# First expert in 64 slots with unsplit products and its rows in two halves, alone, then three split blocks to two of pairs

## The chip, the cores and the metric

The kernel runs on one core of a Trainium2 chip. The metric is the device time of one execution in microseconds (us). Before the change the median of three runs is 1375.55 us (1373.21 to 1376.93). TensorE is called PE here, VectorE DVE, ScalarE ACT, GpSimd POOL, and SP is the engine whose queue issues nearly all loads.

## What is computed

Two decoder layers over 256 positions of width 1024 in float32. The even layer is two kinds of attention and a dense SwiGLU. The odd layer is a mixture of dilated attentions and then a mixture of experts, which is where the change lies:

```python
def expert_block(args):
    xb, e = args
    return (jax.nn.silu(xb @ w1[e]) * (xb @ w3[e])) @ w2[e]
```

A router takes for each of the 256 positions the two experts of eight with the highest logits; each expert is a SwiGLU of inner width 3584 over the positions that chose it, and the two results are summed with the softmax of the two logits. Every expert's w1 and w3 are 1024x3584 and w2 is 3584x1024, so all eight hold 352 MB, and each word is needed once. With the reference's own inputs the router sends 63, 71, 67, 71, 63, 63, 60 and 54 rows to experts 0 to 7 (worked out by running the reference).

## The kernel before

**Places and slots.** After the router the experts are sorted by their row counts, the largest first, but expert 0 is always put at place 0, because its weights can then be loaded before the router has answered (`picked(0)` names `W[n][0]`; for other places SP reads the expert's number into a register). `CAP` gives the slots of each place: 128 for places 0 to 3, 64 for places 4 to 7. An expert with more rows than slots is finished by `overflow`, a loop under an If that is not entered with these counts.

**Blocks.** An expert's work is cut into seven blocks of 512 inner columns. A block needs six weight tiles of 1 MB: two of w1, two of w3 (each 4 x 128 rows by 512 columns), two of w2 (2 x 128 rows by 1024). `load` takes the next of twelve slots in a fixed round (six of the `raw` pool, then buffers that the attention has left, listed in `late`) and issues the DMA on SP; the DMA waits until that slot's last reader is done.

**Two kinds of blocks.** A *split* block (places 0 to 3, 128 slots) writes each weight as hi + lo: ACT rounds a row of 1024 to `hi` (line 222), DVE takes the rest to `lo` (line 223), and PE makes three matmuls of it (`mm3`, lines 232 to 234). Only five pairs of hi and lo exist (`WB=5`). A *pair* block takes two experts of 64 slots at once (`up2`, line 285; `down`, line 651): unsplit float32 matmuls straight from the raw tiles, one expert on columns 0 to 63 of the array and one on columns 64 to 127, side by side. Each such matmul stands twice in a trace.

**Order.** `swiglu` walks the list `items`. For each item it makes x.w1, takes silu on ACT (line 700), finishes the item before (transposes in `gate_T`, then w2 in `down`), makes x.w3 and multiplies on DVE (line 713). The list is split, split, pair, fourteen times; the last pair block is cut into two of 256 columns. Before an expert's first block `begin` gathers its rows with one-hot matrices (lines 973 and 979), after its last `combine` scatters them back. `overflow` stands in item 26.

**Ahead.** Expert 0's first two w1 tiles are loaded and split during the attention of the odd layer by `ahead`, with POOL doing the subtraction.

Of the kernel before, what the change touches and what calls it, by code (L numbers as in the profile page):

```python
# [7 lines left out]
F32 = mybir.dt.float32  # L8
# [30 lines left out]

CAP = (128, 128, 128, 128, 64, 64, 64, 64)  # L40
FIRST = 1 << 20
# [111 lines left out]
def trunk(ctx: ExitStack, tc: tile.TileContext, a, out, R=6, WB=5, NF=16):  # L153
# [462 lines left out]
    def swiglu(items, ws, between=None, behind=None, next_ws=None, tail=None, rare=None):  # L616
# [22 lines left out]
        def down(it, gs, fill=iter(())):  # L639
            w1, w3, w2, c0, n, sta, accs, first, last, pre, post = it  # L640
            nr = n // P
            accs = accs()
            if isinstance(w1, tuple):
# [14 lines left out]
                return  # L658
            for r in range(0, nr, 2) if not last else [0]:
                ws = []  # L660
                m = 1 if tail and it is items[-1] else 2
                for q in range(r, nr if last else r + 2, m):
                    v = load(w2, c0 // P + q, m, 0, D)
                    ws += [split(v[:, j:j + 1, :]) for j in range(m)]
# [13 lines left out]
        for it in items:  # L678
# [13 lines left out]
            two = isinstance(w1, tuple)  # L692
            u = up2(p1[0], w1, c0, n, sta[0]) if two else up(p1, w1, c0, n, sta, ws, between)
            step(u, 2)
            if prev:
# [3 lines left out]
            for q, p in zip(s, p1):  # L699
                A.activation(q[:, :n], p[:, :n], AF.Silu)  # L700
            held = tail and it is items[-1]
            if prev and not held:
                down(prev[0], gs)
            if rare and it is items[26]:
                rare()
            p3 = [wk() for _ in sta]
            with tc.issue_after(behind) if ws else nullcontext():
                end(up2(p3[0], w3, c0, n, sta[0]) if two else up(p3, w3, c0, n, sta))
            ws = None
            if held:  # L710
                down(prev[0], gs)
            for q, p in zip(s, p3):
                V.tensor_mul(q[:, :n], q[:, :n], p[:, :n])  # L713
            prev = (it, s)
# [97 lines left out]
    for i, m in enumerate(mms):  # L812
        TE.matmul(pc[:, :8], lhsT=upb[:, P:], rhs=m, start=i == 0, stop=i == len(mms) - 1)
    over, place = [cp.tile([P, 8], F32, name=q) for q in ("over", "place")]
    tmp = fa("tmp")
# [14 lines left out]
    with tc.issue_after(behind):  # L830
# [6 lines left out]
        V.tensor_copy(number, place[0:1, :])  # L837
        V.tensor_tensor(over, m8, cst[:, C_LIM:C_LIM + 8], op=ALU.is_gt)
        V.tensor_reduce(mx, over[0:1, :], axis=AX, op=ALU.max)
        V.tensor_copy(most, mx)  # L840
# [40 lines left out]
    state = {}  # L881

    new_y = lambda: xp.tile([P, 2, D], F32R, tag="x", name=nm("y"), bufs=2)

    def overflow():

        ws = [raw() for _ in range(2)]
        fs = [fa("more") for _ in range(4)] + [fb("more") for _ in range(2)]
        ys, m = new_y(), fs[3]
        with tc.If(nc.values_load(most, min_val=0, max_val=1) > 0):  # L890

            nth, n = [m[:, 8 * i:8 * i + 8] for i in range(2)]
            V.tensor_copy(n[:, 0:1], over[:, 0:1])
            for i in range(1, N_EXP):
                V.tensor_add(n[:, i:i + 1], n[:, i - 1:i], over[:, i:i + 1])
# [5 lines left out]
    def more(nth, m, wa, xg, wd0, wd1, g, _, fo, fg, ys):  # L901
# [3 lines left out]
        one, t, col, t2 = [m[:, 8 * i:8 * i + 8] for i in range(4)]  # L905
        V.tensor_scalar(one, nth, 1.0, None, op0=ALU.is_equal)

# [13 lines left out]
        pick(col[:, 5:6], t2)  # L921
        for h in range(2):
            pick(col[:, h:h + 1], slots[h])
# [41 lines left out]

    def gather(qs):

        n = len(qs) * P
        oneh = fb("oneh")[:, :2 * n].rearrange("p (h j s) -> p h j s", h=2, s=P)
        for h in range(2):  # L970
            for j, q in enumerate(qs):
                s = slot0[h][:, 0:1] if q == 0 else slots[h][:, q:q + 1]
                V.tensor_scalar(oneh[:, h, j, :], iota, s, None, op0=ALU.is_equal)
        xg = []
        for k in range(KT):
            ps = wk()
            for i, xs in enumerate((xh, xl)):
                for h in range(2):
                    TE.matmul(ps[:, i * n:(i + 1) * n], lhsT=xs[h][:, k * P:(k + 1) * P],
                              rhs=oneh[:, h].rearrange("p j s -> p (j s)"), start=h == 0, stop=h == 1)  # L980
            yield
            if k * n % T == 0:
                t = fb("xg")
            v = t[:, k * n % T * 2:][:, :2 * n]
            (A.copy if k % 2 else V.tensor_copy)(v, ps[:, :2 * n])
            xg.append(v.rearrange("p (a s) -> p a s", a=2))
        for j, q in enumerate(qs):
            ssl = slice(j * P, (j + 1) * P)
            state["sta", q] = [lambda k, ssl=ssl: (xg[k][:, 0, ssl], xg[k][:, 1, ssl])]
            state["oneh", q] = oneh[:, :, j, :]  # L990

# [20 lines left out]

    def begin(qs):

        if CAP[qs[0]] == 64:
            yield from gather2(qs[0])
        elif ("sta", qs[0]) not in state:
            yield from gather(qs)
        q = qs[0]
        n = P // CAP[q]  # L1020
        state["ot", q] = by_slot(state["oneh", q], [g[:, q:q + n, :].rearrange("p a b -> p (a b)") for g in gg], n,
# [40 lines left out]
    def picked(q):  # L1062
# [11 lines left out]
        return [Picked(n, a[n], ROWS[n], at) for n in ("odd_w1", "odd_w3", "odd_w2")]  # L1074


    def expert(q):
        end_ = q == 6
        ch = [(c, 512) for c in range(0, D_FFE, 512)]
        if end_:  # L1080
            ch[-1:] = [(D_FFE - 512, 256), (D_FFE - 256, 256)]
        ws3 = list(zip(picked(q), picked(q + 1))) if CAP[q] == 64 else picked(q)
        for i, (c, n) in enumerate(ch):
            first, last = i == 0, i == len(ch) - 1
            pre = None
            if first:
                pre = lambda: begin([q])
            elif (q, i) == (0, 1):
                pre = residual
            yield (*ws3, c, n, lambda: state["sta", q], lambda: e_acc(q), first, last, pre,  # L1090
                   (lambda: combine(q, end_)) if last else None)
# [62 lines left out]
```

## Time and profile before

| what | value |
|---|---|
| median of the runs | 1375.55 us |
| the profiled execution's own time | 1373.32 us |
| its span (first to last instruction) | 1371.6 us |
| busy: PE, DVE, ACT | 1300.7, 784.7, 614.1 us |
| mean HBM traffic over the span | 310 GB/s |
| first matmul of the experts | at 470.12 us |
| last weight tile landed | by 1350 us (2 GB/s from there to 1357.5 us) |

Times inside a trace are us from the span's start. A span is read with care: PE counts as busy while matmuls overlap, so a PE at 95% is not a PE at its peak. The experts take from 470 us to the end, and the DMA engines move all their weights in that time, so both have to be read by stretches.

### The profile page before, as it was taken

To read this page: it belongs to the slowest core of one execution; us is meant where nothing else is said; L and a number is where in the kernel's file an instruction comes from. 1 tells how busy PE (TensorE), PEld (TensorE's weight loads), DVE (VectorE), ACT (ScalarE), POOL (GpSimd) and SP (SyncE) were. 2 spreads that over 40 slices of the span, in tenths; PEclk is the share of its full clock that TensorE was granted. 3 is DMA by queue.
4 is the path that set the end of the run, shared out by engine and by line. 5 is a ranking of instruction groups with operands and counts; after the bars stand their busy time and mean duration, and the time that the engine had idled before them with its cause. 6 is when DMAs were issued, how large, how long until landed. Compare 5 with 4: busy or idle time off the path is not lost. (4 is left out here: it accounts for less than half of the span.)

```text
span 1371.6 us, 16690 instructions
## 1 busy us (share of the span) xinstructions
PE 1300.7 (95%) x6130; PEld 886.3 (65%) x6130; DVE 784.7 (57%) x1201; ACT 614.1 (45%) x859; POOL 53.7 (4%) x40
## 2 busy tenths in 40 slices
PE   9998999999999899999999999999979999999996
PEld 7776888887777775564746556466646475646562
DVE  6988445547777574453645455464625474644463
ACT  5564434443555364453444445254525353544441
POOL 0012000101022100000000000000000000000001
PEclk9999999999999699999999999999999999999998
DMA  9532456654445489999999999997999998999964
GB/s 371 193 110 98 161 184 222 224 194 158 154 148 184 168 308 399 422 419 422 408 376 422 419 421 404 384 359 288 423 366 384 416 412 346 420 420 421 401 230 168
DMA packets 69191, 426.23 MB, mean 311 GB/s; under 512 B 7920, under 2 KB 16368, under 8 KB 19824
## 3 DMA queue, kind: packets, MB, share of 16 engines
q1 hardware_dynamic: 68096, 421.70, 78.0%
q0 software_dynamic: 864, 3.15, 0.7%
q8 instruction: 50, 0.82, 0.2%
q14 instruction: 37, 0.30, 0.1%
q10 hardware_dynamic: 144, 0.26, 0.1%
HBM read 424.03 MB, written 1.05 MB: 310 GB/s over the span
## 5 line engine op out<-in xcount | busy, mean ns | idle before, releaser
L223 DVE TENSOR_TENSOR lo<-raw,hi 128x1024 fp32r<-128x1024 f32 (+1 forms) x454 | 535.0, 1219 | 236.6 <-ACT hi L222 235.7
L222 ACT ACTIVATE hi<-raw 128x1024 fp32r<-128x1024 f32 (+2 forms) x472 | 467.1, 1034 | 230.6 <-PE wk L234 124.1
L285 PE MATMUL wk<-raw,xg 128*64 128x512 f32 (+1 forms) x960 | 213.1, 575 | 5.5 <-PEq L890 5.3
L233 PE MATMUL wk<-lo,xg 128*128 128x512 f32 x448 | 177.8, 397 | 5.3 <-DVE lo L223 5.2
L232 PE MATMUL wk<-hi,xg 128*128 128x512 f32 x448 | 178.3, 398 | 0.5 <-DVE x L1057 0.5
L234 PE MATMUL wk<-hi,xg 128*128 128x512 f32 x448 | 175.2, 391 | 0.0
L713 DVE TENSOR_TENSOR sl<-sl,wk 128x512 f32<-128x512 f32 (+1 forms) x55 | 36.3, 666 | 227.3 <-PE wk L285 139.3
L285 PEld LDWEIGHTS wk<-raw,xg 128*64 128x64 f32 x960 | 69.2, 138 | 128.1 <-issue 121.6
L232 PE MATMUL acc<-hi,gh 128*128 128x512 f32 x312 | 118.5, 400 | 15.1 <-ACT hi L222 14.5
L233 PE MATMUL acc<-lo,gh 128*128 128x512 f32 x312 | 122.7, 395 | 4.7 <-DVE lo L223 4.7
L234 PE MATMUL acc<-hi,gl 128*128 128x512 f32 x312 | 121.6, 392 | 1.4 <-DVE gl L635 1.2
L232 PEld LDWEIGHTS wk<-hi,xg 128*128 128x128 f32 x448 | 84.4, 188 | 37.2 <-issue 19.5
L233 PEld LDWEIGHTS wk<-lo,xg 128*128 128x128 f32 x448 | 84.4, 188 | 26.3 <-DVE lo L223 8.9
L651 PE MATMUL acc<-raw,gt 128*64 128x512 f32 x448 | 100.9, 598 | 0.3 <-ACT gt L626 0.3
L234 PEld LDWEIGHTS wk<-hi,xg 128*128 128x128 f32 x448 | 84.4, 188 | 16.9
L700 ACT ACTIVATE sl<-wk 128x512 f32<-128x512 f32 (+1 forms) x55 | 32.0, 582 | 138.4 <-PE wk L285 74.3
L232 PEld LDWEIGHTS acc<-hi,gh 128*128 128x128 f32 x312 | 58.0, 188 | 36.5 <-ACT hi L222 22.0
L232 PE MATMUL wk<-hi,xT 128*128 128x512 f32 (+1 forms) x192 | 72.4, 377 | 0.3 <-ACT xT L315 0.3
L233 PEld LDWEIGHTS acc<-lo,gh 128*128 128x128 f32 x312 | 58.6, 188 | 21.7 <-DVE lo L223 9.4
L233 PE MATMUL wk<-lo,xT 128*128 128x512 f32 (+1 forms) x192 | 71.7, 373 | 0.0
L234 PE MATMUL wk<-hi,xT 128*128 128x512 f32 (+1 forms) x192 | 71.5, 373 | 0.0
L651 PEld LDWEIGHTS acc<-raw,gt 128*64 128x64 f32 x448 | 35.2, 137 | 54.7 <-issue 54.0
(208 smaller groups left out, 1359.3 us busy)
## 6 DMA issues: line engine op xcount, KB each, us to landing
raw<-in_odd_w SPq DMA_DIRECT2D x326, 1024.0 KB, 9.6
raw<-in_even_w SPq DMA_DIRECT2D x31, 1024.0 KB, 4.9
raw<-in_odd_w_in SPq DMA_DIRECT2D x12, 1024.0 KB, 4.8
raw<-in_odd_w SPq DMA_DIRECT2D x20, 512.0 KB, 5.4
raw<-in_even_w_in SPq DMA_DIRECT2D x8, 1024.0 KB, 11.7
raw<-in_even_w_out SPq DMA_DIRECT2D x4, 1024.0 KB, 5.4
raw<-in_odd_w_out SPq DMA_DIRECT2D x4, 1024.0 KB, 5.2
raw<-in_even_w SPq DMA_DIRECT2D x4, 512.0 KB, 3.6
```

The source lines that it names most:

```text
L222: A.activation(hi, v, AF.Copy)
L223: by.tensor_sub(lo, v, hi.bitcast(F32))
L232: TE.matmul(o, lhsT=sh, rhs=wh, start=first, stop=False)
L233: TE.matmul(o, lhsT=sh, rhs=wl, start=False, stop=False)
L234: TE.matmul(o, lhsT=sl, rhs=wh, start=False, stop=last)
L285: TE.matmul(o[i * 64:(i + 1) * 64, :ncol], lhsT=sta(r + k, i), rhs=v[:, k, :], start=r + k == 0, stop=r + k == KT - 1)
L651: TE.matmul(accs[0][d][i * 64:(i + 1) * 64, :], lhsT=gs[:, s], rhs=w[:, j, d * 512:(d + 1) * 512], start=first and r + j == 0, stop=last a ...
L700: A.activation(q[:, :n], p[:, :n], AF.Silu)
L713: V.tensor_mul(q[:, :n], q[:, :n], p[:, :n])
```

## The change

Expert 0 gets 64 slots and a third kind of block. Its matmuls are unsplit, like a pair's, but with no second expert to stand beside it the two column halves of the array take two halves of its own contraction: rows 0 to 511 of the weights on columns 0 to 63, rows 512 to 1023 on columns 64 to 127 (`up1`). The two partial sums lie in PSUM one above the other. They are copied out (ACT for w1's, DVE for w3's) and added while they are turned, by a matmul with `fold`, two identities of 64 one above the other; silu and the product follow (`gate_T`). In w2 the halves are the inner rows, and the two partial results are scattered by a doubled one-hot. `fold` and the count column `over` lie in attention masks that are no longer read.

The list of items becomes: seven blocks of expert 0, then seven rounds of split, pair, split, split, pair. The last pair block is no longer cut in two. For a pair block after a split one, the split block's w2 tiles are loaded and split first (`rows_of`), ahead of the pair's w1. The tiles split ahead during the attention are gone, and all twelve slots are filled with raw tiles instead. Overflow moves to item 23; expert 0 with 65 to 192 rows now counts as overflowing once, with more twice.

```diff
-CAP = (128, 128, 128, 128, 64, 64, 64, 64)
+CAP = (64, 128, 128, 128, 64, 64, 64, 64)
...
+    def up1(o, w, c0, ncol, sta):
+        vs = [load(w, r, 4, c0, ncol) for r in (0, 4)]
+        for k in range(4):
+            for i, v in enumerate(vs):
+                TE.matmul(o[i * 64:(i + 1) * 64, :ncol], lhsT=sta(4 * i + k), rhs=v[:, k, :], start=k == 0, stop=k == 3)
+            if k % 2:
+                yield
...
         def gate_T(it, g):
             n = it[4]
+            if isinstance(it[0], list):
+                pt, t = wk(), fa("gt")
+                for i, q in enumerate(g):
+                    for j in range(n // P):
+                        TE.matmul(pt[:, i * T + j * 64:i * T + (j + 1) * 64], lhsT=q[:, j * P:(j + 1) * P], rhs=fold,
+                                  start=True, stop=True)
+                A.activation(t[:, :T], pt[:, :T], AF.Silu)
+                V.tensor_mul(t[:, :T], t[:, :T], pt[:, T:])
+                return t
...
+            if isinstance(w1, list):
+                ws = [load(w2[0], c0 // P + r, 2, 0, D) for r in (0, 2)]
+                for j in range(2):
+                    for d in range(2):
+                        for i, w in enumerate(ws):
+                            s = slice((2 * i + j) * 64, (2 * i + j + 1) * 64)
+                            TE.matmul(accs[0][d][i * 64:(i + 1) * 64, :], lhsT=gs[:, s], rhs=w[:, j, d * 512:(d + 1) * 512],
+                                      start=first and j == 0, stop=last and j == 1)
...
-                m = 1 if tail and it is items[-1] else 2
-                for r in range(0, nr, m):
+                for r, m in ((0, 2), (2, 1), (3, 1)) if tail and it is items[-1] else ((0, 2), (2, 2)):
...
+            rows = list(rows_of(prev[0])) if two and prev and isinstance(prev[0][0], Tiles) else None
...
-            if rare and it is items[26]:
+            if rare and it is items[23]:
...
-    ws = ahead(w1[0], 0, 512)
...
-    ws += ahead(w1[0], 0, 512, 4)
-    late += ["raw"] * 4 + ["qT", "kT", "vv", "oh", "ol"] + ["raw"] * (R - 4) + ["x"]
+    late += ["raw"] * R + ["qT", "kT", "vv", "oh", "ol", "x"]
...
+    def gather1():
...
+        xg, ps = fa("xg"), wk()
+        for k in range(KT):
+            for i, xs in enumerate((xh[0], xh[1], xl[0], xl[1])):
+                TE.matmul(ps[:, k * 64:(k + 1) * 64], lhsT=xs[:, k * P:(k + 1) * P], rhs=oneh[:, i % 2, :64],
+                          start=i == 0, stop=i == 3)
+        V.tensor_add(fold, ident[:, :64], ident[:, 64:])
...
-    alone, paired = run(*(expert(q) for q in range(4))), run(expert(4), expert(6))
-    items = []
-    for it in alone:
-        items += [it, next(alone), next(paired)]
-    items += paired
-    swiglu(items, ws, behind=behind, tail=sums, rare=overflow)
+    items = list(expert(0))
+    split_, paired = run(*(expert(q) for q in range(1, 4))), run(expert(4), expert(6))
+    for it in split_:
+        items += [it, next(paired), next(split_), next(split_), next(paired)]
+    swiglu(items, None, behind=behind, tail=sums, rare=overflow)
```

**PE, start of the experts.** Here stands before the end of the gather (line 979), the turned one-hots (1028, 1030) and the first split products (232 to 234):

```order
L979 MATMUL wk_4137<-oneh_4088,xT_3912 128x128
L1028 MATMUL wk_4145<-cst,oneh_4088 128x128 x2
L1030 MATMUL wk_4145<-gg_4067,oneh_4088 128x2
L1030 MATMUL wk_4145<-gg_4085,oneh_4088 128x2
L232 MATMUL wk_4153<-hi_3519,xg_4096 128x512
L233 MATMUL wk_4153<-lo_3520,xg_4096 128x512
L234 MATMUL wk_4153<-hi_3519,xg_4096 128x512
```

In the changed kernel the same place reads (line 1046 is the gather, 295 is `up1`):

```order
L1046 MATMUL wk_4066<-oneh_4060,xT_3884 128x64
L1087 MATMUL wk_4104<-cst,oneh_4060 128x128
L1089 MATMUL wk_4104<-gg_4039,oneh_4060 128x2
L1089 MATMUL wk_4104<-gg_4057,oneh_4060 128x2
L295 MATMUL wk_4112<-raw_4113,xg_4065 64x512
L295 MATMUL wk_4112<-raw_4115,xg_4065 64x512
L295 MATMUL wk_4112<-raw_4113,xg_4065 64x512
```

The gather's outputs are half as wide, and each 128 rows of weights are one matmul from the raw tile where they were three from hi and lo.

**PE, between two blocks of expert 0 in the changed kernel.** Line 635 is the fold, 678 is w2:

```order
L295 MATMUL wk_4200<-raw_4203,xg_4065 64x512
L635 MATMUL wk_4213<-cst,sl_4169 128x64 x4
L635 MATMUL wk_4213<-cst,sl_4198 128x64 x4
L295 MATMUL wk_4239<-raw_4240,xg_4065 64x512
L295 MATMUL wk_4239<-raw_4242,xg_4065 64x512
L295 MATMUL wk_4239<-raw_4240,xg_4065 64x512
L678 MATMUL acc_4171<-raw_4227,gt_4214 64x512
```

The eight fold matmuls are new, and some matmuls of the next w3 stand between them and w2. At this place the kernel before has split blocks, with four transposes (line 632) and the three matmuls of `mm3`.

**ACT, a pair block after a split block (the one with the If).** Before, hi tiles of the next w3, the split block's turned gate (`gh`), the pair's silu (`sl`), and only then the four hi tiles of the split block's w2:

```order
L222 ACTIVATE hi_7744<-raw_7732 128x1024
L634 ACTIVATE gh_7773<-wk_7768 128x512
L700 ACTIVATE sl_7789<-wk_7755 128x512
L222 ACTIVATE hi_7793<-raw_7791 128x1024
L222 ACTIVATE hi_7797<-raw_7791 128x1024
L222 ACTIVATE hi_7815<-raw_7813 128x1024
L222 ACTIVATE hi_7819<-raw_7813 128x1024
```

and in the changed kernel:

```order
L222 ACTIVATE hi_6667<-raw_6655 128x1024
L222 ACTIVATE hi_6681<-raw_6679 128x1024
L222 ACTIVATE hi_6685<-raw_6679 128x1024
L222 ACTIVATE hi_6691<-raw_6689 128x1024
L222 ACTIVATE hi_6695<-raw_6689 128x1024
L652 ACTIVATE gh_6716<-wk_6711 128x512
L739 ACTIVATE sl_6732<-wk_6678 128x512
```

The four hi tiles of w2 moved from behind the silu to ahead of it.

## Rows read from the trace of the kernel before

**Rows 1.** Windows: us, busy time and count by engine, PEclk, DMA share, GB/s.
```profile
475.00:1350.00 875.00, 835.61 (x3772) 518.38 (x3770) 455.66 (x472) 384.47 (x445) 0.00 (x0) 1.00 0.95 385
550.00:600.00 50.00, 50.00 (x225) 29.87 (x223) 22.84 (x22) 21.93 (x24) 0.00 (x0) 1.00 1.01 421
475.00:530.00 55.00, 54.34 (x264) 37.89 (x262) 32.69 (x38) 30.06 (x33) 0.00 (x0) 1.00 0.83 315
680.00:690.00 10.00, 10.00 (x48) 5.38 (x48) 1.92 (x3) 1.43 (x2) 0.00 (x0) 1.00 0.66 238
885.00:955.00 70.00, 67.40 (x322) 43.27 (x320) 38.86 (x51) 30.41 (x38) 0.00 (x0) 1.00 0.83 309
1005.00:1035.00 30.00, 21.68 (x81) 9.60 (x78) 6.91 (x7) 7.22 (x9) 0.00 (x0) 0.89 0.87 329
1130.00:1145.00 15.00, 15.00 (x71) 8.92 (x71) 6.78 (x7) 5.21 (x6) 0.00 (x0) 1.00 0.69 255
1310.00:1350.00 40.00, 37.02 (x211) 23.04 (x210) 16.30 (x19) 10.53 (x15) 0.00 (x0) 1.00 0.70 248
```
**Rows 2.** Issues of loads: line, engine, count, size, median us from issue to landing.
```profile
raw<-in_odd_w SPq DMA_DIRECT2D x326, 1024.0 KB, 9.6
```
**Rows 3.** Chain that ended last, one round of split, split, pair: start, us, what.
```profile
1034.61 0.50 PE wk L233
...
1071.45 7.03 PE wk L285 x30
...
1078.99 1.06 ACT hi L222
1080.07 1.24 DVE lo L223
1081.35 0.50 PE acc L233
...
1086.65 7.07 PE wk L285 x32
...
1094.35 1.23 DVE lo L223
1095.62 0.50 PE wk L233
```
**Rows 4.** Timeline from the router to the first expert matmul: start, us, engine, line.
```profile
443.99 1.95 PE L773 MATMUL acc<-rt,x3T 128*128 128x8 f32 x16 [0.60 <-ACT x3T L770]
...
456.64 1.22 DVE L223 TENSOR_TENSOR lo<-raw,hi 128x1024 fp32r<-128x1024 f32 x1
459.21 0.15 DVE L837 CAST number<-place 1x8 int32<-1x8 f32 x1
460.28 1.21 DVE L223 TENSOR_TENSOR lo<-raw,hi 128x1024 fp32r<-128x1024 f32 x1
462.43 7.17 PE L979 MATMUL wk<-oneh,xT 128*128 128x128 f32 x32 [4.51 <-DVE oneh L973]
470.12 0.77 PE L232 MATMUL wk<-hi,xg 128*128 128x512 f32 x1
```
**Rows 5.** Windows around the If of overflow, and behind the last load, columns as in rows 1.
```profile
1005.00:1017.00 12.00, 9.84 (x41) 5.49 (x38) 4.63 (x4) 6.39 (x7) 0.00 (x0) 1.00 0.94 375
1017.00:1022.70 5.70, 0.42 (x2) 0.01 (x1) 0.00 (x0) 0.00 (x0) 0.00 (x0) 0.91 0.79 323
1021.70:1028.50 6.80, 5.78 (x14) 1.91 (x16) 0.00 (x0) 0.00 (x0) 0.00 (x0) 0.50 0.78 290
1350.00:1357.50 7.50, 7.50 (x34) 2.54 (x32) 0.00 (x0) 0.00 (x0) 0.00 (x0) 1.00 0.01 2
```
**Rows 6.** Timeline of PE behind the If.
```profile
1022.72 9.95 PE L285 MATMUL wk<-raw,xg 128*64 128x512 f32 x32 [5.30 <-PEq L890]
```
**Rows 7.** Chain at the end: the last w2 products, start, us, what.
```profile
1350.43 7.11 PE acc L651 x32
```
**Rows 8.** Timeline of POOL: issuing one DMA.
```profile
448.15 0.60 POOL L304 DMA_DIRECT2D gb<-in_odd_ln_g  x1
```

More of the change, by code (lines that the diff above doesn't have):

```diff
@@ L637, in gate_T, with rows_of, down @@
             return gs
-        def down(it, gs, fill=iter(())):
+        def rows_of(it):
+            w2, c0, n, last = it[2], it[3], it[4], it[8]
+            nr = n // P
+            for r in range(0, nr, 2) if not last else [0]:
+                ws = []
+                for q in range(r, nr if last else r + 2, 2):
+                    v = load(w2, c0 // P + q, 2, 0, D)
+                    ws += [split(v[:, j:j + 1, :]) for j in range(2)]
+                yield r, ws
+        def down(it, gs, fill=iter(()), rows=None):
             w1, w3, w2, c0, n, sta, accs, first, last, pre, post = it
@@ L658, in down @@
                 return
[L659 to L664, printed above, removed]
+            for r, ws in rows or rows_of(it):
                 for i, (gh, gl) in enumerate(gs):
@@ L692, in swiglu @@
             two = isinstance(w1, tuple)
-            u = up2(p1[0], w1, c0, n, sta[0]) if two else up(p1, w1, c0, n, sta, ws, between)
-            step(u, 2)
+            rows = list(rows_of(prev[0])) if two and prev and isinstance(prev[0][0], Tiles) else None
+            one = isinstance(w1, list)
+            u = up2(p1[0], w1, c0, n, sta[0]) if two else up1(p1[0], w1[0], c0, n, sta[0]) if one else up(p1, w1, c0, n, sta, ws, between)
+            step(u, 3 if prev and isinstance(prev[0][0], tuple) else 2)
             if prev:
@@ L699, in swiglu @@
             for q, p in zip(s, p1):
-                A.activation(q[:, :n], p[:, :n], AF.Silu)
+                A.activation(q[:, :n], p[:, :n], AF.Copy if one else AF.Silu)
             held = tail and it is items[-1]
             if prev and not held:
-                down(prev[0], gs)
-            if rare and it is items[26]:
+                down(prev[0], gs, rows=rows)
+            if rare and it is items[23]:
                 rare()
@@ L707, in swiglu @@
             with tc.issue_after(behind) if ws else nullcontext():
-                end(up2(p3[0], w3, c0, n, sta[0]) if two else up(p3, w3, c0, n, sta))
+                end(up2(p3[0], w3, c0, n, sta[0]) if two else up1(p3[0], w3[0], c0, n, sta[0]) if one else up(p3, w3, c0, n, sta))
             ws = None
             if held:
-                down(prev[0], gs)
-            for q, p in zip(s, p3):
-                V.tensor_mul(q[:, :n], q[:, :n], p[:, :n])
+                down(prev[0], gs, rows=rows)
+            if one:
+                s.append(fa("sl"))
+                V.tensor_copy(s[1][:, :n], p3[0][:, :n])
+            else:
+                for q, p in zip(s, p3):
+                    V.tensor_mul(q[:, :n], q[:, :n], p[:, :n])
             prev = (it, s)
@@ L813, in trunk @@
         TE.matmul(pc[:, :8], lhsT=upb[:, P:], rhs=m, start=i == 0, stop=i == len(mms) - 1)
-    over, place = [cp.tile([P, 8], F32, name=q) for q in ("over", "place")]
+    place = cp.tile([P, 8], F32, name="place")
+    over = cst[:, C_D1:C_D1 + 9]
     tmp = fa("tmp")
@@ L881, in trunk @@
     state = {}
+    fold = cst[:, C_D0:C_D0 + 64]
     new_y = lambda: xp.tile([P, 2, D], F32R, tag="x", name=nm("y"), bufs=2)
@@ L890, in overflow @@
         with tc.If(nc.values_load(most, min_val=0, max_val=1) > 0):
-            nth, n = [m[:, 8 * i:8 * i + 8] for i in range(2)]
+            nth, n = [m[:, 16 * i:16 * i + 9] for i in range(2)]
             V.tensor_copy(n[:, 0:1], over[:, 0:1])
-            for i in range(1, N_EXP):
+            for i in range(1, N_EXP + 1):
                 V.tensor_add(n[:, i:i + 1], n[:, i - 1:i], over[:, i:i + 1])
@@ L921, in more @@
         pick(col[:, 5:6], t2)
+        V.scalar_tensor_tensor(col[:, 5:6], col[:, 7:8], float(P), col[:, 5:6], op0=ALU.mult, op1=ALU.add)
         for h in range(2):
@@ L964, in more_block, with gather @@
                 V.tensor_add(y[:, c], y[:, c], ps)
-    def gather(qs):
-        n = len(qs) * P
-        oneh = fb("oneh")[:, :2 * n].rearrange("p (h j s) -> p h j s", h=2, s=P)
+    def gather(q):
+        oneh = fb("oneh")[:, :2 * P].rearrange("p (h s) -> p h s", h=2)
         for h in range(2):
-            for j, q in enumerate(qs):
-                s = slot0[h][:, 0:1] if q == 0 else slots[h][:, q:q + 1]
-                V.tensor_scalar(oneh[:, h, j, :], iota, s, None, op0=ALU.is_equal)
+            V.tensor_scalar(oneh[:, h, :], iota, slots[h][:, q:q + 1], None, op0=ALU.is_equal)
         xg = []
@@ L978, in gather @@
                 for h in range(2):
-                    TE.matmul(ps[:, i * n:(i + 1) * n], lhsT=xs[h][:, k * P:(k + 1) * P],
-                              rhs=oneh[:, h].rearrange("p j s -> p (j s)"), start=h == 0, stop=h == 1)
+                    TE.matmul(ps[:, i * P:(i + 1) * P], lhsT=xs[h][:, k * P:(k + 1) * P], rhs=oneh[:, h, :],
+                              start=h == 0, stop=h == 1)
             yield
-            if k * n % T == 0:
+            if k % 2 == 0:
                 t = fb("xg")
-            v = t[:, k * n % T * 2:][:, :2 * n]
-            (A.copy if k % 2 else V.tensor_copy)(v, ps[:, :2 * n])
+            v = t[:, k % 2 * T:][:, :T]
+            (A.copy if k % 2 else V.tensor_copy)(v, ps[:, :T])
             xg.append(v.rearrange("p (a s) -> p a s", a=2))
[L987 to L990, printed above, removed]
+        state["sta", q] = [lambda k: (xg[k][:, 0, :], xg[k][:, 1, :])]
+        state["oneh", q] = oneh
+    def gather1():
+        oneh = fb("oneh")[:, :2 * P].rearrange("p (h s) -> p h s", h=2)
+        for h in range(2):
+            for j in range(2):
+                V.tensor_scalar(oneh[:, h, j * 64:(j + 1) * 64], iota[:, :64], slot0[h][:, 0:1], None, op0=ALU.is_equal)
+        xg, ps = fa("xg"), wk()
[4 more added lines that the diff above has]
+        V.tensor_add(fold, ident[:, :64], ident[:, 64:])
+        A.copy(xg[:, :256], ps[:, :256])
+        V.tensor_copy(xg[:, 256:], ps[:, 256:])
+        yield
+        state["sta", 0] = [lambda k: xg[:, k * 64:(k + 1) * 64]]
+        state["oneh", 0] = oneh
     def gather2(q):
@@ L1011, in gather2, with begin @@
         state["oneh", q] = oneh
[L1013 to L1020, printed above, removed]
+    def begin(q):
+        yield from gather2(q) if q > 3 else gather(q) if q else gather1()
+        n = 2 if q > 3 else 1
         state["ot", q] = by_slot(state["oneh", q], [g[:, q:q + n, :].rearrange("p a b -> p (a b)") for g in gg], n,
```

30 lines of the change are left out of this document (17 added, 13 removed).

## Prediction

> **What bounds the kernel now.** The experts' stretch comes first, as a whole and then by pieces [rows 1]. From 475 to 1350 us the loads run at 385 GB/s on average. Where nothing holds them, 550 to 600 us, they run at 421 GB/s and the DMA share is 1.01: that is the ceiling here. So of 875 us the loads lose 875 x (1 - 385/421) = 75 us. The reader is to see where: by the same formula the start (475 to 530) loses 13.8 us, the switch from expert 0 to place 1 4.3 (680 to 690), the switches to place 2 and to the second pair, which coincide, 18.6 (885 to 955), the If of overflow 6.6 (1005 to 1035), place 3 5.9 (1130 to 1145), the end 16.4 (1310 to 1350). That is 65.6; some 9 us are spread thin. Outside the holes PE is nearly always busy too, at full clock [rows 1].
>
> Next the size of the cushion: a tile lands 9.6 us after its issue [rows 2], and at 421 GB/s a tile of 1.0486 MB takes 2.49 us, so about four of the twelve slots are in flight and the others hold landed tiles. PE lags, and a PE delay of some 7 us empties the queue.
>
> Last a round of split, split, pair [rows 3]: 1034.61 to 1095.62, 61.0 us. Its 24 tiles take 59.8 us of DMA. On PE two waits stand in it: from 1071.45 + 7.03 to 1081.35, 2.9 us, in which ACT makes hi only after the pair's silu and DVE lo after that; and from 1086.65 + 7.07 to 1095.62, 1.9 us, for lo of the next split block. PE's own work is 61.0 - 4.8 = 56.2 us: a pair is 3 x 7.07 and about 0.6 of transposes, 21.8; a split block is (56.2 - 21.8)/2 = 17.2 against 14.9 us of its six tiles. Split blocks are PE's, pairs the loads', and the two add up to nearly the same. Hence PE never gains on its backlog, and every extra delay turns into a hole.
>
> **The change, part by part.** *Start.* Two lo products of DVE that stand ahead of the one-hots go, 1.2 each [rows 4], and the gather's 32 matmuls (7.17 us at the low clock) have half the columns: between 3.6 and 7.2, I take 4.5, since the weight loads stay as wide; a last copy costs 0.5 that was overlapped. 470.1 - 2.4 - 2.7 + 0.5 gives 465.5, say 466. The tiles that POOL split ahead are no longer there: 12 tiles are landed by then, where before it were 14.7 (of 336, less 875 us x 385 GB/s = 336.9 MB). The first slots come free when w1's two tiles are used, about 5 us at the low clock: 471. SP's register loads of the eight numbers now stand ahead of the 13th tile, but the numbers are cast by 459.4 [rows 4] and the tile's slot isn't free before 471: nothing.
>
> *Expert 0.* A matmul pair of halves is what a pair block has, 32 records in 7.07 us [rows 3]; a block has 48 records, 10.6 us. The fold is eight float32 matmuls with short moving sides; the nearest row is the router's, 16 records in 1.95 us [rows 4], so 2.0. The silu and product behind it are covered by matmuls of the next w3 in PE's order; without that cover they cost at most what ACT and DVE take there for widths of 1024, 1.06 + 1.24 [rows 3], 16 us for seven blocks. 12.6 us a block, 88 for seven, 2 for the low clock: done at 466 + 90 = 556, where a split expert took 7 x 17.2 = 120. The loads need 30 further tiles, 471 + 75 = 546, so they stay ahead and run full.
>
> *Rounds.* Split, pair, split, split, pair has 42 tiles, 104.6 us. On PE: 3 x 17.2 + 2 x 21.8 = 95.2, plus 1.9 after each pair; the 2.9 goes, because w2's hi and lo now stand ahead of the silu (they hold four of five hi/lo pairs during the pair's first product, and the next split block needs them only behind w2, so nothing waits). 99.0 us: PE has 5.6 us to spare per round, where before it had none.
>
> *Switches and If.* From 470.1 to the end of w2's products, 1350.43 + 7.11 = 1357.5 [rows 7], PE took 887.4 us; fourteen rounds are 854; 33 remain for five gathers with their combines, the cold start and the If, which costs 5.3 of standing still and 9.95 - 7.07 = 2.9 at the low clock [rows 6]. I keep the 33. The switches no longer coincide: they come at the first split and pair, and in rounds 3, 4 and 5.
>
> *End.* The last pair block isn't cut, so the last twelve slots hold whole tiles, not halves. That should close most of the hole of 16.4.
>
> **The sum, twice.** PE: 556 + 7 x 99.0 + 33 = 1282. Loads: 471 + 324 tiles x 2.49 = 471 + 807 = 1278; plus holes. The If's 6.6 stays, the thin 9 stays; of the 28.8 us at switches I keep a quarter, 7, for PE's spare time pays back one switch of 4 to 5 us per round; of the end 3. That is 1304 for the last landing. Behind it stand 8.5 us of PE (the last landing of before is put at 1349, since from 1350 on 2 GB/s are left [rows 5], to 1357.5) and 14.1 to the end of the span (1371.6 - 1357.5). 1326.6. The loads set the end, PE by some 20 us not. The profiled execution took 1.7 us more than its span, and the median of the runs is 2.2 above that execution: 1326.6 + 3.9 = 1330.5, I say **1330 us**, 3.3% less. A measurement of this kernel can tell about 0.3% from no change.
>
> From both sides: no hole at all but the start's, 1278 + 8.5 + 14.1 + 3.9 = 1305. All holes as before, except the start's, 61 us: 1366.
>
> **The rivals.** *The holes stay.* If PE keeps lagging (two adjacent split blocks need twelve lo each on DVE, 12 x 1.24 = 14.9 us, as long as their loads), the switches and the end cost what they cost: 1366. For it: PE is busy almost throughout. Against: it has spare time now. 10%.
>
> *The clock falls; slower.* Expert 0 gives PE 12.6 us of work per 14.9 us of loads, once the twelve tiles are used up, so PE stands and waits at each tile. If the clock goes to its low level there, a block takes up to twice 12.6, 25 us; seven at that level add 88 us, PE becomes the bound, 1282 + 88 + 14.1 + 3.9 = 1388: slower than 1375.5 by 0.9%. Break-even is near six of the seven blocks at the low clock. For it: the clock did fall to its 1.2 GHz level [rows 5], behind 5.7 us in which PE did nothing. Against: in the 12 us before, with PE busy 82% of the time and waiting in between, it stayed at 2.4 GHz, and a PE at half clock would have no gaps and so no cause to stay there. The Trainium skill has a rule that speaks for this rival: its page "TensorE: Matmul & The Clock Gate", section "HAM oscillation — how this bites in real kernels", tells of a kernel whose work per weight tile was shorter than the wait for the next and which lost the fast clock on every tile; by it the 1388 would be the forecast, while the rows above bear it out only for a full stop. 5%.
>
> *Expert 0 overflows; the change then doesn't do what it says.* With a 65th row the If is entered: 28 pieces with six loads each from POOL, at least 28 x 6 x 0.6 = 101 us of issuing [rows 8], so 1430 or more. It decides at 65 rows and the reference sends 63. 2%.
>
> **How the numbers follow.** Forecast, 1305 to 1350: 0.81. Holes stay, 1350 to 1366: 0.10. Clock: 0.05. Overflow: 0.02. 0.02 for something that I don't see. The range leaves out about 2 in 10: 1306 to 1358. Below 1305 the ceiling of 421 GB/s stands. Faster by over 0.3%: 0.91 (the forecast and the holes); within: 0.03; slower: 0.06.
>
> **What would show it.** The first matmul of line 295 near 466 us; the granted clock at full from about 472 to 560 us; loads at 420 GB/s from there with no hole at the first switch; rounds of 104 to 107 us; the If still a hole of 6 to 9 us; hi of w2 ahead of the pair's silu and no wait of 2.9 us; the last tile landing near 1304 us and the span ending 23 us later. Wrong would be: blocks of expert 0 over 15 us long, loads below 400 GB/s between 480 and 560 us, rounds of 107 us or more, or matmuls inside the If.

## The result and the profile after

The changed kernel takes 1342.36 us (median of 4 runs, 1339.68 to 1344.62), the kernel before 1375.72 us in the same runs: a ratio of 0.9759, 95% interval 0.9731 to 0.9787. The forecast was 1330 us in a range of 1306 to 1358: the direction and the range hold, and 12 us are missing. The profiled execution took 1344.62 us with a span of 1343.0 us.

Windows of the changed kernel, columns as in [rows 1]: the first block's start, the start of the loads, the rest of expert 0, the first switch (first for its clock, then for its loads), a stretch of rounds, a later switch, the end, and the whole.

```profile
466.00:472.00 6.00, 6.00 (x16) 3.45 (x18) 0.74 (x3) 0.49 (x2) 0.00 (x0) 0.54 0.00 0
472.00:480.00 8.00, 8.00 (x41) 4.76 (x37) 0.69 (x1) 1.88 (x2) 0.00 (x0) 1.00 0.80 309
480.00:553.00 73.00, 72.07 (x365) 33.30 (x365) 5.99 (x11) 5.45 (x12) 0.00 (x0) 1.00 1.01 416
557.00:564.00 7.00, 7.00 (x26) 4.23 (x27) 2.78 (x3) 2.66 (x4) 0.00 (x0) 0.52 1.01 417
585.00:600.00 15.00, 14.71 (x77) 8.86 (x78) 2.00 (x6) 1.15 (x3) 0.00 (x0) 1.00 0.61 241
700.00:850.00 150.00, 147.47 (x638) 84.48 (x638) 71.89 (x76) 61.87 (x74) 0.00 (x0) 1.00 1.01 421
957.00:990.00 33.00, 32.54 (x163) 22.03 (x164) 17.15 (x24) 15.13 (x19) 0.00 (x0) 1.00 0.80 298
1306.00:1329.00 23.00, 22.09 (x83) 7.46 (x81) 4.01 (x6) 1.38 (x3) 0.00 (x0) 1.00 0.04 15
475.00:1306.00 831.00, 811.02 (x3564) 458.06 (x3561) 360.22 (x388) 305.17 (x362) 0.00 (x0) 0.99 0.99 409
```

The loads run at 409 GB/s where they ran at 385, so of the 75 us that they lost some 24 are left, 831 x (1 - 409/421). (The GB/s are the last column, the share of the fast clock that PE was granted the third from the end.) The holes of the If and of the end [rows 1] are gone, that of the start nearly; a tile now lands 12.4 us after its issue (9.6 before [rows 2]), so more transfers wait in the queue. What has come in their place stands in the row before the last: from 1306 to 1329 us next to nothing is loaded, and PE is busy for 22.1 of 23 us. The chain of the changed kernel's end (start, us, what) shows with what:

```profile
1306.40 3.58 PE wk L285 x14
...
1314.72 3.59 PE wk L285 x14
1318.34 0.70 DVE sl L756
...
1320.60 3.58 PE acc L692 x16
1324.18 1.06 PE wk L919 x2
1325.24 3.68 PE acc L692 x16
1328.91 0.68 ACT y L1108
```

The last tile has landed near 1306 us, and PE still stands in the last pair's w3 (line 285; DVE's product at 1318.34 waits for its end), in between products that combine an expert, with the pair's w2 (line 692) still ahead of it; in the kernel before only w2 was left then [rows 5, 7]. That is a backlog of PE. The list of PE's waits (line, releaser, us in total, times, longest) says the same of the time before; these are all groups of over 0.3 us from 600 to 1306 us:

```profile
PE wk L233 <- DVE lo L223: 8.0, 13, 2.4
PE wk L643 <- DVE sl L756: 5.0, 11, 0.5
PE wk L285 <- PEq L936: 1.5, 1, 1.5
```

No load is among them. The waits for hi and lo of w2 [rows 3] are gone, as forecast. Yet a round takes longer than forecast. The timeline of PE at one pair, where the split block's w2 now stands ready:

```profile
1185.81 1.07 PE L285 MATMUL wk<-raw,xg 128*64 128x512 f32 x2
1186.81 0.66 PE L650 MATMUL wk<-cst,sl 128*128 128x128 f32 x4
1187.40 3.65 PE L285 MATMUL wk<-raw,xg 128*64 128x512 f32 x14
1190.97 0.50 PE L232 MATMUL acc<-hi,gh 128*128 128x512 f32 x1
1191.31 0.40 PE L233 MATMUL acc<-lo,gh 128*128 128x512 f32 x1
1191.63 1.07 PE L285 MATMUL wk<-raw,xg 128*64 128x512 f32 x2
1192.64 0.50 PE L234 MATMUL acc<-hi,gl 128*128 128x512 f32 x1
...
1195.13 3.65 PE L285 MATMUL wk<-raw,xg 128*64 128x512 f32 x14
1198.71 0.50 PE L232 MATMUL acc<-hi,gh 128*128 128x512 f32 x1
...
1201.65 7.09 PE L285 MATMUL wk<-raw,xg 128*64 128x512 f32 x32
```

From 1185.81 to 1201.65 PE makes the pair's w1 (32 records) and the split block's w2 (24), woven into each other: w1 falls into four pieces. Two records alone hold PE for 1.0 us (1191.63 to 1192.64), against 0.44 in an unbroken run of 32 in 7.07. The kernel before made w1 in one run and then waited:

```profile
1069.79 1.07 PE L285 MATMUL wk<-raw,xg 128*64 128x512 f32 x2
...
1071.38 7.08 PE L285 MATMUL wk<-raw,xg 128*64 128x512 f32 x30
1080.09 0.73 PE L232 MATMUL acc<-hi,gh 128*128 128x512 f32 x2 [1.63 <-ACT hi L222]
1081.35 0.50 PE L233 MATMUL acc<-lo,gh 128*128 128x512 f32 x1 [0.53 <-DVE lo L223]
...
1086.58 0.65 PE L285 MATMUL wk<-raw,xg 128*64 128x512 f32 x2
```

16.8 us there, 15.8 here: of the 2.9 us that the split ahead was to take away, about 1 was left. (PE's idle time in them is only 1.63 + 0.53 us, the numbers in brackets; two products of w2 stand in between.) The order that the scheduler gives PE has changed: w2 is ready early now, and it puts w2's products among those of the pair's second two w1 tiles. That it does so because it expects these tiles late is an inference; a run below with smaller tiles fits it, and no run shows it.

### The profile page after: what moved, and what is told of

Same layout as the page of the kernel before. It is cut to its first block, busy times and chain, and to the rows that moved or that the text cites. A ratio compares the mean times of both kernels' runs of the same rounds, so it can differ in the third digit from the quotient of the medians.

```text
span 1343.0 us, 16136 instructions
## 1 busy us (share of the span) xinstructions
PE 1293.2 (96%) x5982; PEld 830.7 (62%) x5982; DVE 688.4 (51%) x1121; ACT 530.6 (40%) x768; POOL 41.4 (3%) x34
## 5 line engine op out<-in xcount | busy, mean ns | idle before, releaser
L223 DVE TENSOR_TENSOR lo<-raw,hi 128x1024 fp32r<-128x1024 f32 (+2 forms) x374 | 439.1, 1214 | 159.1 <-ACT hi L222 157.8
L222 ACT ACTIVATE hi<-raw 128x1024 fp32r<-128x1024 f32 (+2 forms) x386 | 383.5, 1035 | 200.0 <-PE wk L234 114.1
L285 PE MATMUL wk<-raw,xg 128*64 128x512 f32 x896 | 229.9, 598 | 1.5 <-PEq L936 1.5
L233 PE MATMUL wk<-lo,xg 128*128 128x512 f32 x336 | 134.0, 399 | 8.0 <-DVE lo L223 8.0
L232 PE MATMUL wk<-hi,xg 128*128 128x512 f32 x336 | 134.6, 401 | 0.0
L234 PE MATMUL wk<-hi,xg 128*128 128x512 f32 x336 | 131.9, 392 | 0.0
L234 PE MATMUL acc<-hi,gl 128*128 128x512 f32 x256 | 101.2, 397 | 0.3 <-DVE gl L653 0.2
L233 PE MATMUL acc<-lo,gh 128*128 128x512 f32 x256 | 100.3, 392 | 0.0
L232 PEld LDWEIGHTS wk<-hi,xg 128*128 128x128 f32 x336 | 63.4, 189 | 32.3 <-issue 18.9
L233 PEld LDWEIGHTS wk<-lo,xg 128*128 128x128 f32 x336 | 63.5, 189 | 24.6 <-DVE lo L223 11.6
L234 PEld LDWEIGHTS wk<-hi,xg 128*128 128x128 f32 x336 | 63.5, 189 | 12.6
L232 PE MATMUL acc<-hi,xT 128*128 128x512 f32 (+1 forms) x172 | 69.0, 401 | 0.9 <-ACT xT L324 0.9
L234 PE MATMUL acc<-hi,xT 128*128 128x512 f32 (+1 forms) x172 | 67.3, 392 | 0.2 <-DVE xT L325 0.2
## 6 DMA issues: line engine op xcount, KB each, us to landing
raw<-in_odd_w SPq DMA_DIRECT2D x334, 1024.0 KB, 12.4
```

What stands on the lines that cost most here:

```text
L222: A.activation(hi, v, AF.Copy)
L223: by.tensor_sub(lo, v, hi.bitcast(F32))
L232: TE.matmul(o, lhsT=sh, rhs=wh, start=first, stop=False)
L233: TE.matmul(o, lhsT=sh, rhs=wl, start=False, stop=False)
L234: TE.matmul(o, lhsT=sl, rhs=wh, start=False, stop=last)
```

## Experiments

Two theories were set against each other. **A:** PE sets the pace of the changed kernel to the end, and the weave is a part of its load. **B:** the loads set it, as the prediction had it, and PE only the 22 us behind them. All times are medians; the kernel before took 1374.5 to 1376.8 us beside them.

**Split ahead taken back.**

```diff
-            rows = list(rows_of(prev[0])) if two and prev and isinstance(prev[0][0], Tiles) else None
+            rows = None
```

> The changed kernel, but a split block's w2 tiles are again loaded and split behind the pair's silu; all else as changed. In the changed kernel the stretch of PE from the pair's first w1 product to the split block's last w2 product is 15.84 us (1185.81 to 1201.65): 7.07 and 5.44 of products, 0.6 of transposes, and 2.7 more, because w1 and w2 are woven there, float32 and split products in turn. In the kernel before the same stretch had w1 in one piece and the wait of 2.9 us, 16.8 us in all. Theory A (PE sets the pace everywhere from 466 us on; what the split ahead won, 2.9 us, it gave back by the weave): 14 pairs x 1.0 us, some 13 us slower than the changed kernel, 1353 to 1358. Theory B (the loads set the pace until 1306 us, PE only the 22 us behind it): the wait is hidden as far as PE has time to spare, within 5 us of the changed kernel, 1338 to 1347. What the prediction assumed (2.9 us gone, nothing in its place) would make it 14 x 2.9 = 41 us slower if PE is the bound.

Measured: 1360.1 us (1357.2 to 1363.2), 17.7 more than the changed kernel. That is A's direction and a little above its figure; B's 1347 and the 41 us of the prediction's step both fail. The waits are back, w1 is again in one run, and a plain round takes 105.0 us where it took 103.2 (from one start of a pair's w2 to the next but one):

```profile
PE acc L232 <- ACT hi L222: 16.3, 10, 1.6
PE acc L233 <- DVE lo L223: 6.6, 11, 1.3
```

The 17.7 us aren't a clean price of that, though. At one place PE stood 5.0 us for a tile, and the 32 products behind it took 10.03 us where they take 7.09 at the full clock; here are they and the window behind the wait, with a granted clock of 0.51. These 8 us stand in neither theory.

```profile
930.37 10.03 PE L285 MATMUL wk<-raw,xg 128*64 128x512 f32 x32 [5.04 <-DMA raw<-in_odd_w]
930.30:936.50 6.20, 6.13 (x16) 2.05 (x18) 0.00 (x0) 0.00 (x0) 0.00 (x0) 0.51 0.88 307
```

**PE's order held.** The split ahead stays; w2's products are ordered behind w1's last one, the pair's w3 behind w2's last.

```diff
+                    pe[0] = m.ins
...
-                            mm3(accs[i][d], gh[:, s], gl[:, s], wh[:, 0, c], wl[:, 0, c],
-                                first and r + j == 0, last and r + j == nr - 1)
+                            with tc.issue_after(pe[0]) if rows else nullcontext():
+                                mm3(accs[i][d], gh[:, s], gl[:, s], wh[:, 0, c], wl[:, 0, c],
+                                    first and r + j == 0, last and r + j == nr - 1)
+            if rows:
+                pe[0] = pe[1]
...
-            with tc.issue_after(behind) if ws else nullcontext():
+            with tc.issue_after(behind) if ws else tc.issue_after(pe[0]) if rows else nullcontext():
```

> The changed kernel with PE's order held at each pair: the split block's w2 products stand behind the pair's last w1 product, the pair's w3 behind w2's last; the split ahead stays. Theory A (PE is the bound and the weave costs it 2 to 2.7 us per pair): 14 x 2 to 2.7 = 28 to 38 us of PE go, of which the loads let through what is in their holes and in the wait behind the last landing, so 1310 to 1325. Theory B (the loads are the bound): the last landing stays at 1306 us, and only the last pair's 2 us are won, 1338 to 1342.

Measured: 1326.0 us (1325.3 to 1331.1), 16.4 less than the changed kernel with the same products, loads and slots, ratio to the kernel before 0.9650 (0.9628 to 0.9672). That is 1 us above A's range and far outside B's. PE at one pair, and two windows of the end:

```profile
1172.38 1.07 PE L287 MATMUL wk<-raw,xg 128*64 128x512 f32 x2
...
1173.97 7.08 PE L287 MATMUL wk<-raw,xg 128*64 128x512 f32 x30
1180.98 0.50 PE L234 MATMUL acc<-hi,gh 128*128 128x512 f32 x1
...
1186.67 1.51 PE L287 MATMUL wk<-raw,xg 128*64 128x512 f32 x6
```

```profile
475.00:1290.00 815.00, 789.12 (x3565) 454.42 (x3562) 359.87 (x387) 306.40 (x361) 0.00 (x0) 1.00 1.00 414
1290.00:1297.00 7.00, 7.00 (x31) 5.13 (x29) 1.44 (x2) 0.99 (x2) 0.00 (x0) 1.00 0.74 300
1297.00:1310.00 13.00, 13.00 (x51) 4.38 (x49) 3.23 (x5) 1.18 (x3) 0.00 (x0) 1.00 0.00 1
```

The stretch is 14.3 us against 15.84: the weave costs 1.55 us. It stands at 12 of the 14 pairs (at two, begun at 593.48 and 980.83 in the changed kernel, w1 and w3 run unbroken in both), 18.6 us of PE, and 16.4 show in the time. A plain round takes 100.1 us, 103.2 in the changed kernel: two weaves less. The list of PE's waits now has a load in it:

```profile
PE wk L287 <- DMA raw<-in_odd_w: 4.6, 4, 1.3
```

**The first lo besides.** As the last run, and the first piece of a split block behind a pair is loaded and split before the pair's product, so that DVE makes two lo ahead of it (PE waits for lo there, 1.9 us with the transposes' wait [rows 3]).

```diff
+                first_ = [next(more_), next(more_)]
+                head = run(first_, more_)
+                sub = lo_[0]
...
+                    with tc.issue_after(sub) if sub else nullcontext():
+                        V.tensor_mul(q[:, :n], q[:, :n], p[:, :n])
```

> As the run with PE's order held, and besides the first two lo of the split block behind a pair are made on DVE ahead of the pair's product with w3, so that PE doesn't wait 1.9 us at each of those places. Theory A: up to 13 x 1.9 = 25 us more off PE; PE's path would then end at about 1329 - 30 - 25 = 1275, ahead of the loads, so the loads become the bound at 1278 to 1290 for the last landing plus 10 to 20 us of PE and 14.1 us of end: 1305 to 1322, and no more than 10 us below the run without it. Theory B: as that run, 1338 to 1342.

Measured: 1326.2 us, nothing won, above A's 1305 to 1322 and below B's 1338. The 1.9 us were no measure of the wait: PE's idle time at such a place of the changed kernel is 0.45 us before the transposes and 0.48 before the lo product, with work between. PE's waits for lo fell from 7.6 to 3.1 us and its waits for loads rose from 4.6 to 13.1. So with w1 in one run and lo first the loads are the bound; by these runs the distance between the two bounds in the changed kernel was some 16 us.

**Last pair cut in two.**

```diff
+        if q == 6:
+            ch[-1:] = [(D_FFE - 512, 256), (D_FFE - 256, 256)]
...
+    items += paired
```

> The changed kernel with its last pair block cut in two of 256 columns again, as in the kernel before. Theory A (at the end PE has a backlog of its own work; whole tiles only let the loads finish earlier): the last landing comes some 10 us later, PE behind it shrinks by as much, and the time stays within 3 us of the changed kernel or is up to 5 us above it, for the cut pieces add changes of kind on PE: 1340 to 1348. Theory B (the 22 us behind the last landing come from the uncut tiles, and cut ones would bring 8.5 us back): 1328 to 1334.

Measured: 1343.4 us, A. The hole at the end is back (272 GB/s from 1290 to 1320 us) and what PE does behind the last landing, now near 1320 us, is w2 alone, which ends at 1328.46 us (1328.92 in the changed kernel). The window, and w2 in the chain:

```profile
1290.00:1320.00 30.00, 29.17 (x174) 16.73 (x173) 9.40 (x13) 3.45 (x7) 0.00 (x0) 1.00 0.76 272
...
1321.35 7.11 PE acc L693 x32
```

**The old order of the list.**

```diff
+    alone, paired = run(*(expert(q) for q in range(4))), run(expert(4), expert(6))
+    items = []
+    for it in alone:
+        items += [it, next(alone), next(paired)]
```

> The changed kernel with the list of items as before, two blocks of places 0 to 3 and one pair in turn, so that expert 0's unsplit blocks stand between pairs; all else as changed. Theory A (PE sets the pace): a round of two blocks of expert 0 and a pair needs 2 x 12.4 + 21.8 = 46.6 us of PE and 59.8 us of loads, so in three and a half such rounds PE uses up the landed tiles and waits for some 22 us, which nothing gives back; 3 weaves of 2.7 us and 3 waits of 1.9 us fall away, since no split block stands beside those pairs. So 1345 to 1360, slower than the changed kernel. Theory B (the loads set the pace): the order doesn't matter to them, 1338 to 1346.

Measured: 1352.0 us, 9.6 above the changed kernel, within A. PE waits for tiles between expert 0's blocks (145.57 us busy of 160 from 480 to 640 us) and, by A, lacks that time later; no run took that apart.

**Expert 0's tiles loaded twice.**

```diff
+        vs2 = [[load(w, r, 4, c0, ncol) for r in (0, 4)] for _ in range(2)]
...
+                ws2 = [[load(w2[0], c0 // P + r, 2, 0, D) for r in (0, 2)] for _ in range(2)]
```

> The changed kernel, but each weight tile of expert 0 is loaded twice, into two slots, and each copy is used for half of the products. A block of expert 0 then needs 29.9 us of loads for 12.4 us of PE, and PE waits at each tile. If the clock stands such waits, the granted clock stays at 1.00 from 480 us to the end of expert 0 at about 650 us and the time is that of 42 more tiles less PE's lead, 1342 + 97, 1430 to 1450 us. If the prediction's rival is right one step further out (PE standing at each tile loses the fast clock), the clock shows 0.5 in that stretch and the blocks take up to 25 us of PE, still behind the loads, so the clock tells it, not the time.

Measured: 1441.2 us, within the expected time. PE stood at 30 of the upward loads for up to 1.9 us and at 20 of w2's for up to 0.7. The granted clock lay between the two cases expected: 0.97 as the mean of the stretch, for it fell to 0.50 three times (near 518.6, 583.5 and 638.1 us), some 10 us in all, and stood at 1.00 otherwise. The stretch and a piece of the first fall:

```profile
480.00:640.00 160.00, 117.02 (x354) 35.54 (x354) 5.99 (x11) 5.77 (x12) 0.00 (x0) 0.97 1.01 422
519.00:522.00 3.00, 3.00 (x8) 0.74 (x4) 0.00 (x0) 0.00 (x0) 0.00 (x0) 0.50 1.02 423
```

```profile
PE wk L295 <- DMA raw<-in_odd_w: 31.5, 30, 1.9
```

**Held order, and the last pair cut besides** (both diffs above).

> The run with w1 in one piece, with the last pair block cut in two of 256 columns besides. There the loads are the bound: the last tile lands at 1296 us and PE works 14 us behind it. Theory A: cutting didn't matter while PE had a backlog (1343.4 against 1342.4), but here it does: what stands behind the last landing falls towards the 8.5 us of the kernel before, 1318 to 1323. Rival (cut pieces make nothing shorter, or their smaller transfers are slower): 1325 to 1330.

Measured: 1326.8 us against 1326.0: nothing, as the rival had it, so A's expectation failed. PE's work of the last pair is the same, cut or not, and its products ended at 1311.7 us, 1309.8 without the cut.

**Held order without the If.**

```diff
-    swiglu(items, None, behind=behind, tail=sums, rare=overflow)
+    swiglu(items, None, behind=behind, tail=sums)
```

> The run with w1 in one piece, without overflow's If; this leaves out the part for experts with more rows than slots, which isn't entered with these counts. The prediction kept 6.6 us of the loads' time for the If: 1319 to 1321 if so. Against it the trace of that run: PE stands 2.7 us at the If and the loads run at 419 to 422 GB/s around it: 1323 to 1327.

Measured: 1324.4 us (1321.7 to 1325.1), 1.5 less than with the If, within the scatter and within the second range. The 6.6 us that the prediction kept for it aren't there.

**Half of the pairs' w1 and w3 not loaded**, in the changed kernel and with PE's order held.

```diff
-            vs = [load(w, r, 4, c0, ncol) for w in ws]
+            vs = [load(w, r, 2, c0, ncol) for w in ws]
```

> The changed kernel, but of each w1 and w3 tile of a pair block only half is loaded, and each half is used twice; the products are the same in number and size. This leaves half of the pairs' w1 and w3 weights out. The loads become 14 x 8 halves shorter, 56 x 2.49 = 139 us. Theory A (PE sets the pace from 466 us to the end): nothing is won but what the holes cost, 1336 to 1344. Theory B (the loads set the pace): PE's own path comes to light; by the prediction that is 1282 + 14.1 + 3.9 = 1300.

> The same halved loads with PE's order held as in the run with w1 in one piece; half of the pairs' w1 and w3 weights are left out. This tells how far PE's own path lies below the loads there. In that run PE waits for loads for 4.6 us in all: so 1319 to 1325 if these are all that the loads cost it. If the loads cost it more, through landings that come late without a wait put down to them, 1305 to 1318.

Measured: 1305.0 and 1304.5 us. By the numbers the first would speak for B. It doesn't, for the edit moved more than the loads: with smaller tiles the scheduler wove nothing, as the timeline of PE shows, and also set lo ahead of the pair's product (PE's waits for lo are 2.9 us, 2 times, where the changed kernel has 8.0, 13 times).

```profile
1157.06 1.07 PE L285 MATMUL wk<-raw,xg 128*64 128x512 f32 x2
...
1158.65 7.08 PE L285 MATMUL wk<-raw,xg 128*64 128x512 f32 x30
1165.66 0.50 PE L232 MATMUL acc<-hi,gh 128*128 128x512 f32 x1
```

So this run doesn't part A from B. What the two tell is PE's own path without weave and with few waits for lo: 1304.5 us. The run with the held order and the first lo besides has the same two and whole loads, and takes 21.7 us more: so much the loads cost there. Against the held order alone it is 21.5 us, but there PE also waits for lo; a plain round takes 97.3 us in both runs with half loads and 100.1 there.

**Rounds of split, split, pair, split, pair**, with PE's order held, and then with the first lo besides. The If stands at item 24 there.

```diff
-        items += [it, next(paired), next(split_), next(split_), next(paired)]
+        items += [it, next(split_), next(paired), next(split_), next(paired)]
```

> The run with w1 in one piece, its rounds in the order split, split, pair, split, pair, so that the first pair's gather no longer stands right behind place 1's. In that run 5 to 6 us of loads are lost at 585 to 600 us, where both switches coincide, and some 7 us at 970 us. If two switches side by side are what empties the queue, the first hole shrinks and the time falls by 2 to 6 us: 1320 to 1324. If PE's backlog alone does it, the hole moves and nothing changes: 1324 to 1329.

> As the run before in this list, and the first two lo of a split block behind a pair are made ahead of the pair's product, which takes 1.9 us off PE at each such place. With PE lighter than the loads and the two switches apart, both holes should shrink: 1315 to 1322. If the loads' own length (807 us from 473 us), the first switch and PE's work behind the last landing are all there is, it stays with the others at 1324 to 1328.

Measured: 1323.4 us (0.9617, 0.9602 to 0.9633) and 1320.9 us (0.9605, 0.9586 to 0.9624). The second is the fastest of the runs that load all weights, 21 us below the changed kernel and 5 below the held order alone, intervals apart; the first lies in the range of the switches pulled apart, but is too near the held order to tell. The reason given for it was half wrong: the hole at the first switch moved and grew, the one at 970 us went, and so it is in the second run (297 GB/s from 600 to 616 us). First the held order, then the first of these two runs:

```profile
585.00:600.00 15.00, 15.00 (x76) 7.38 (x77) 2.71 (x7) 3.36 (x5) 0.00 (x0) 1.00 0.81 323
967.00:980.00 13.00, 13.00 (x68) 6.93 (x68) 1.31 (x5) 0.95 (x3) 0.00 (x0) 1.00 0.53 193
```

```profile
603.00:616.00 13.00, 13.00 (x70) 7.71 (x70) 1.31 (x5) 0.38 (x1) 0.00 (x0) 1.00 0.46 170
967.00:980.00 13.00, 13.00 (x63) 5.21 (x63) 1.08 (x5) 2.87 (x4) 0.00 (x0) 1.00 0.98 398
```

## Why the prediction was right in direction and 12 us short

**Start: right by luck, through two errors that cancel.** The first expert matmul came at 466.16 us, forecast 466. But the gather's 32 matmuls took 7.2 us (31 of them 6.80), the upper bound and not the 4.5 chosen, and they began 3.9 us earlier than in [rows 4] where 2.4 was forecast. Loads were issued from 472.5 us instead of 471.

**Expert 0: right.** The fold took 2.00 us as forecast, and from one fold to the next, 528.91 to 541.29, a block is 12.4 us (forecast 12.6). The clock stayed at 1.00 (window 480 to 553), so the rival of the falling clock did not come true. But the prediction argued it on a false premise: PE never waited for a load in expert 0, since the twelve landed tiles lasted to its end. The run with each tile loaded twice made the premise true: PE waited at 50 of 84 tiles, up to 1.9 us, and the clock fell three times, some 10 of 160 us, far from the rival's seven blocks. The Trainium skill's page "TensorE: Matmul & The Clock Gate", section "HAM oscillation — how this bites in real kernels", tells of a kernel that lost the fast clock at its waits for the next tile, at every tile; that run's trace agrees that it can be lost so, but not at every tile. At the longest wait for a load in any run, the 5.0 us with the split ahead taken back, the trace agrees: the clock was 0.51 behind it. In the changed kernel the clock fell at the switch (0.52 from 557 to 564), where expert 0's last w2 ended at 565.6 us; that time is counted with the switches below.

**Rounds: wrong, the step that failed.** Forecast 99.0 us on PE, "the 2.9 goes ... so nothing waits". Measured 103.2, from the lo product behind one pair to the one a round later, in the chain:

```profile
1150.63 0.50 PE wk L233
...
1253.86 0.51 PE wk L233
```

Two pairs at 15.84 instead of 16.8 - 2.9 = 13.9 are 3.9 of the missing 4.2. Of that 2 x 1.55 = 3.1 are the weave. The other 0.8 is a misreading: the 2.9 us held two products of w2, and without wait and weave the stretch is 14.3, so the wait was worth 2.5. The wait did go; the price that took its place was not a wait but PE's order, which the prediction looked at on ACT alone. Seven rounds make 29 us. Of the 5.6 us a round that PE was to have to spare against the loads' 104.6, 1.4 were left.

**Switches: wrong.** Forecast 33 us for all gathers, combines, the cold start and the If; from the end of expert 0's upward products near 554 to 1328.9 there are 775 us, less 7 x 103.2, so 53. The starts of the pairs' w2 tell where: 43.2 + 60.1 us make a plain round, and 1045.41 to 1112.94, with place 3's switch, takes 67.5 instead of 60.1. From 554 to the first pair's w2 at 613.50 it is 60 us, where a split block, a pair's w1 and w3 and expert 0's last w2 would take about 17 + 15 + 4. The first switch thus costs some 24 us, by subtraction; no run took it apart. Some 3 us of it is the low clock, which the profiled execution with the held order did not have there (1.00 from 557 to 564, behind the same products).

**PE's path** by both: 1282 forecast, 1328.9 measured; 29 + 20 - 2. With that "the loads set the end, PE by some 20 us not" falls.

**Last landing: right by luck, 1304 against some 1306, and not for the reason given.** The loads ended there because PE freed the slots at that pace; with PE's order held they end at 1295.

**End: the term that was mis-sized.** 8.5 us of PE behind the last landing, measured some 22. Closing the hole of 16.4 us was booked as a gain while the 8.5 stayed. The run with the cut pair shows that only the sum counts as long as PE has a backlog. The 14.1 us behind it came out exactly (1328.9 to 1343.0).

**The If: wrong, kindly.** PE stood 1.5 us there and no load was lost.

Span: 1326.6 forecast, 1343.0 measured, 16.4 too few: about 2.5 in the landing and 14 behind it. The 3.9 us from span to median were -0.6, which hides 4.5 of it. The run with the held order shows what the left-out price was worth, 16.4 us. That it takes 1326 us, near the forecast, is partly luck: its last tile lands near 1295 us and not at 1304, and PE works some 14 us behind it and not 8.5.

## What to carry to other kernels

Where an edit only makes work ready earlier, look at the order of the engine that was waiting: a scheduler may use the freedom to mix two kinds of products, and the mix may cost most of the wait that was won. When two engines come out within a few per cent of each other, a hole closed on one of them is a gain only if the other's path is shorter by that much; add up both paths to the last instruction, and don't book a closed hole and an unchanged tail together. And an experiment that makes transfers smaller can change the order too: read the order before the time.

## What the runs showed of the hardware

Two records of a float32 product with 64 columns of weights, alone between split products, hold PE for 1.0 us, in a run 0.44. Over the whole order of the experts the held kernel has 138 changes between float32 products with 64 columns and all others, the changed one 192. At a pair the weave has four changes more and costs 1.55 us, 0.39 us each.

The clock fell to 0.50 three times, some 10 us of 160, while PE waited for a load at more than every second tile. Each fall came with the products behind a wait of 1.3 to 1.4 us; the longest wait there, 1.9 us, had none behind it. Behind a wait of 5.0 us it was 0.51. At a switch it fell to 0.52 in the changed kernel and stayed at 1.00 with the order held, with the same listed wait of 1.1 us ahead in both; so the last wait alone doesn't tell whether it falls. Halving a gather's moving columns at the low clock left its time where it was, 7.2 us.
